# Forming the low parts of the down projection's weights with a ScalarE write and an accumulating DMA

## The chip, the cores and the metric

The kernel runs on one core of a Trainium2 chip. The metric is the device time in microseconds of one execution. Three runs of the kernel before took 1912.0, 1912.75 and 1913.21 us; the median is 1912.75 us.

## The reference

One layer of a decoder trunk is computed for 256 tokens of width 2048, in float32: a normalised input goes through one wide projection, a gated linear attention and a dilated attention run beside each other, their gated sum goes through an output projection and is added to x, and a SwiGLU block and a final norm follow. What matters here is the last part:

```
hf = _rmsnorm(x, ffn_norm[l])
gu = hf @ w_ffn_in[l]
gate, up = gu[..., :D_FF], gu[..., D_FF:]
x = x + (jax.nn.silu(gate) * up) @ w_ffn_out[l]
```

D_FF is 5632. The product with w_ffn_out, 5632 x 2048, is the down projection.

## The kernel before

Every large product is done in three passes of TensorE in a reduced 32-bit format (F32R). A weight w is split exactly in two parts, a high part wh (w rounded to the format) and a low part wl = w - wh; the activations have a high and a low part too. A product is high times high, high times low and low times high.

The weights are streamed from HBM. A *unit* is one DMA of 1 MB issued on SyncE's queue into one of three buffers `raw` (L167 to L173). A unit holds two *subs* of 512 KB, 128 partitions by 1024 elements. For each sub, `split` (L175 to L185) has ScalarE write wh from raw, and VectorE write wl as raw minus wh. The buffers wh and wl have five copies each (`LA + 1`, with `LA = 4`). The main loop splits sub i+4 and then multiplies with sub i (`next_split()` and `mains(sub)`, L899 to L915), so the write of sub i+4 has to wait until TensorE is done with sub i-1. When both subs of a unit are split, the unit's buffer is free and the next unit's load is issued (`next_split`, L839 to L845).

The work is a list of jobs, each one product with a block of weights 512 columns wide, in a fixed order. For the SwiGLU block the order is written out at L815 to L822: pairs of jobs with w_ffn_in (gate and up, functions `evac_fgate` and `evac_fup`), and in between three stretches of down jobs (`down`, L810). The first two stretches have four jobs of 8 subs, the last has four jobs of 6 subs: 32 + 32 + 24 = 88 subs. A sub of a down job is used by 12 matmuls: two 128-row tiles of the weights, two tiles of tokens, three passes.

The elementwise work on a finished job runs in its *evacuation*, which is called right after the split of the next job's fifth sub (index 4) and before that job's first matmul. An up job's evacuation occupies ScalarE and VectorE in turn (`fold`, the products with the gate, and the split of the result by `split_act`). The evacuation of a down job of the last stretch has VectorE add to x1, ScalarE square, and GpSimd multiply by the final norm's weights (L799).

The very last job is done one token tile after the other. It goes through its 6 subs with the first 128 tokens alone (6 matmuls per sub), then twice with half of the columns for the other 128 tokens. Its sixth sub (index 5) goes to blocks named h instead of the ring (L179). DMAs of small tensors are issued on GpSimd's queue.

Of the kernel before, what the change touches and what calls it, by code (L numbers as in the profile page):

```python
# [10 lines left out]
F32 = mybir.dt.float32  # L11
F32R = mybir.dt.float32r
AF = mybir.ActivationFunctionType
ALU = mybir.AluOpType
AX = mybir.AxisListType

P = 128
# [11 lines left out]


class HiLo:
    """Four feature tiles of [128, 256] as exact high and low parts, side by side."""

    def __init__(self, tiles):
        self.t = [t.rearrange("p (a w q) -> p a w q", a=2, w=2) for t in tiles]
# [9 lines left out]


class Job:
    """One product with a weight block.

    kind T gives [token, feature]; F and G give [feature, token], G with the product of the low  # L50
    part of the activations in its own half of the bank. `pairs` names the pairs of PSUM banks."""

    def __init__(self, kind, w, row0, nkt, col0, ncols, ktu, acts, evac, pre=None, pairs=None):
        self.pairs = pairs
# [6 lines left out]
def trunk_layer(ctx: ExitStack, tc: tile.TileContext, x, attn_norm, w_in, w_gk_up, b_gk, gla_norm,  # L61
                b_gate, w_branch_gla, w_branch_dil, w_out, ffn_norm, w_ffn_in, w_ffn_out, rel_bias,
                final_norm, onehot, out):
    nc = tc.nc
# [33 lines left out]
        return HiLo([block(tag, j, F32R) for j in (i, i + 1)])  # L98

    def split_act(hl, src):  # L100
        """Splits [128, 4, 256] in SBUF."""
        for i in range(2):
            act(hl.t[i][:, :, 0], src[:, 2 * i:2 * i + 2], AF.Copy)
        for i in range(2):
            nc.vector.tensor_sub(hl.t[i][:, :, 1], src[:, 2 * i:2 * i + 2], hl.t[i][:, :, 0].bitcast(F32))
# [5 lines left out]
    table = [None]  # L111
# [8 lines left out]
            need(func)  # L120
        nc.scalar.activation(o, i, func, **kw)  # L121

# [1 line left out]
    need(AF.Ln)  # L124
    grow = const.tile([16, P], F32, name="grow")
    nc.scalar.dma_start(grow, attn_norm[0].rearrange("(a p) -> a p", p=P))
# [16 lines left out]
    make_identity(nc, ident)  # L143
    epst = const.tile([P, 1], F32, name="epst")
    nc.vector.memset(epst, EPS)
# [1 line left out]
    def add(job):  # L147
        jobs.append(job)
        job.subs = []
# [25 lines left out]
    def split(sub):  # L175
        n, k = sub["job"].ncols, sub["k"]
        src = sub["unit"]["raw"][:, sub["s0"] * n:(sub["s0"] + k) * n]
        if sub["job"] is jobs[-1] and sub["idx"] > LA:
            wh, wl = (block("h", 2 * (sub["idx"] - LA) + i, F32R) for i in range(2))  # L179
        else:  # L180
            wh = ring.tile([P, 1024], F32R, name="wh", tag="wh", bufs=LA + 1)
            wl = ring.tile([P, 1024], F32R, name="wl", tag="wl", bufs=LA + 1)
        act(wh[:, :k * n], src, AF.Copy)
        nc.vector.tensor_sub(wl[:, :k * n], src, wh[:, :k * n].bitcast(F32))  # L184
        sub["w"] = [t[:, :k * n].rearrange("p (a n) -> p a n", a=k) for t in (wh, wl)]  # L185

    def mains(sub, only=None, part=None):
# [46 lines left out]
                    nc.tensor.matmul(dst, st, mv, start=first and i == 0 and j % per_bank == 0,  # L234
                                     stop=last and i == 2, skip_group_check=True)

# [1 line left out]
    queue = deque()  # L238

    def advance(n=1):  # L240
# [8 lines left out]
                return  # L249

    def idle(n):
        """From an elementwise part to the matmul part n steps later."""
        for _ in range(2 * n + 1):
            yield

# [5 lines left out]
            advance()  # L261

    def col_rstd(name, ss, n):
        """1 / sqrt(ss / n + eps) for a small tile, with one Newton step."""
        p, w = ss.shape
        v = const.tile([p, w], F32, name=f"v_{name}", tag=f"v_{name}")
        r = const.tile([p, w], F32, name=f"r_{name}", tag=f"r_{name}")
        t = const.tile([p, w], F32, name=f"t_{name}", tag=f"t_{name}")
        nc.vector.tensor_scalar(v, ss, 1.0 / n, EPS, op0=ALU.mult, op1=ALU.add)
        act(t, v, AF.Ln)  # L270
        act(r, t, AF.Exp, scale=-0.5)
        nc.vector.tensor_mul(t, r, r)
        nc.vector.scalar_tensor_tensor(t, t, -0.5, v, op0=ALU.mult, op1=ALU.mult)
        nc.vector.scalar_tensor_tensor(r, t, 1.5, r, op0=ALU.add, op1=ALU.mult)
        return r

    def row_bcast(name, r):
        """[128 tokens, 2] -> the same values along the free axis of all partitions."""
        pt = ps_b()
        for a in range(2):  # L280
            nc.tensor.transpose(pt[:, a * P:(a + 1) * P], r[:, a:a + 1].to_broadcast([P, P]), ident)
        R = const.tile([P, S], F32, name=name)
        nc.scalar.copy(R, pt[:, :S])
        return R

# [1 line left out]
    def scale_split(hl, pt, gcol, js=range(4)):  # L287
        for j in js:
            act(hl.hi(j), pt[j], AF.Copy, scale=gcol[:, j:j + 1])
# [5 lines left out]
        return [t[:, j * S:(j + 1) * S] for j in range(4)]  # L295

    def to_blocks(tiles, gcol, hl, js, pt):
        """Transposes the feature tiles js of [token, 2, 512], scales by feature and splits exactly."""
        for j in js:
            for a in range(2):  # L300
                nc.tensor.transpose(pt[j][:, a * P:(a + 1) * P], tiles[:, a, j * P:(j + 1) * P], ident)
        yield
        scale_split(hl, pt, gcol, js)
# [5 lines left out]

    env = {}  # L310

# [1 line left out]
    def fold(job, dst, R=None):  # L313
        """dst[:, j] = (high + low accumulator of feature tile j), times the row R of the tokens."""
        n = len(job.acc)
        for j in range(n):
            t = const.tile([P, S], F32, name="fold", tag="fold", bufs=2)
            act(t, job.acc[j][:, S:2 * S], AF.Copy)
            nc.vector.tensor_add(dst[:, j], job.acc[j][:, 0:S], t)
        if R:  # L320
            nc.vector.tensor_mul(dst, dst, env[R][:, None, :].to_broadcast([P, n, S]))
# [7 lines left out]
                                 env[R][:, None, :].to_broadcast([P, 2, S]))  # L329

    def view(key, slot, a, fresh=True):
        """Block `slot` under `key`, seen as [128, a, 1024 / a]."""
        if key not in env:
            env[key] = block("z", slot).rearrange("p (a t) -> p a t", a=a)
        return env[key]

# [1 line left out]
    gctx = ExitStack()  # L338
    gtmp = gctx.enter_context(tc.tile_pool(name="gtmp", bufs=1))
    wgk = gtmp.tile([17, 1024], F32, name="wgk")  # L340
# [7 lines left out]
    nc.vector.memset(inside[:, ::64], 0.0)  # L348

    def g_chunk(lo, hi, slots, base):  # L350
        """Evacuates output-gate columns lo..hi of a half: silu, and the low-rank part past 1024."""
        def go(job):
            for a in range(2):
                c = lo
                while c < hi:
                    sc = env["rstd"][:, a:a + 1]
                    if c >= 1024:
                        act(lrn[:, a], job.acc[a][:, c - lo:hi - lo], AF.Copy, scale=sc)
                        c = hi
                        continue  # L360
                    j = c // 512
                    e = min(hi, (j + 1) * 512)
                    g = view(("g", base + j), slots[j], 2)
                    act(g[:, a, c - j * 512:e - j * 512], job.acc[a][:, c - lo:e - lo],
                                         AF.Silu, scale=sc)
                    c = e
        return go
# [121 lines left out]
        scale_split(hl, [pt[:, f] for f in range(4)], cols[:, 48:52])  # L489
        oglaHL[h] = hl  # L490

# [1 line left out]
    odil = []  # L493
    dctx = ExitStack()
    ftab = dram.tile([8, 3, 384], F32, name="ftab")
# [117 lines left out]
                then()  # L613
        return go

# [1 line left out]
    h_acts = acts_of(hT)  # L617

    def win(kind, col, n, evac, pre=None):
# [28 lines left out]
        push("bias", bias_table())  # L648
    win("T", C_V + 512, 512, evac_t(("v", 1), 1, after_b))

# [1 line left out]
    SL = ((2, 3, 4, 5, 6), (7, 8, 9, 0, 1))  # L652
    for r in range(4):
        sl = SL[r % 2]
# [12 lines left out]
                    push(f"D{r}", dil_head(h, r))  # L667
            win("T", base + 2048, 256, evac_vd(r, g, sl[3 + g // 2], then if g == 2 else None))

# [1 line left out]
    merged = []  # L671

    def evac_gate(key, slot, bcol):
# [32 lines left out]
    turn = [0]  # L706

    def pairs(n):
        """The next n of the four pairs of PSUM banks."""
        p = [(turn[0] + i) % 4 for i in range(n)]  # L710
        turn[0] = (turn[0] + n) % 4
        return p
# [9 lines left out]
        add(Job("G", w_branch_dil, 0, 8, 512 * i, 512, 4, odil_acts, evac_branch(("gb", i), i, True),  # L722
                {0: lambda: drain("D3")}, **kw(False)))

# [1 line left out]
    x1 = []  # L726
    ss1 = const.tile([P, 2, 4], F32, name="ss1")
    ss2 = const.tile([P, 2, 5], F32, name="ss2")
# [37 lines left out]
        add(Job("T", w_out, 0, KT, 512 * c, 512, 4, merged_acts, evac_out(c),  # L766
                {0: reload_x} if c == 0 else None))

# [1 line left out]
    aT = {}  # L770

    def evac_fgate(p):
# [48 lines left out]
            down(4, 4, False)  # L821
    down(8, 3, True)  # L822

# [1 line left out]
    def rows_to_cols(r, n, name):  # L825
        pt = ps_b()
        nc.tensor.transpose(pt[:, 0:n], r, ident[0:n, 0:n])
# [86 lines left out]
        if sub["last"]:  # L914
            pending = sub["job"]  # L915

# [1 line left out]
    tot = const.tile([P, 2], F32, name="tot2")  # L918

    def add_tokens(src, a, q):  # L920
# [40 lines left out]


def _onehot():
    """Row of the bias table (32: masked) for each dilation and each distance -127..256."""
    import numpy as np
    hot = np.zeros((33, 3, 384), np.float32)
    for g, d in enumerate(DILS):
        for i in range(384):
            delta = i - 127
            b = 32  # L970
            if 0 <= delta <= 128 * d and delta % d == 0:
                dist = np.maximum(delta, 1).astype(np.float64)
                b = delta if delta < 16 else min(
                    31, 16 + int((np.log(dist / 16) / math.log(2048 / 16) * 16).astype(np.int64)))
            hot[b, g, i] = 1.0
    return hot
# [21 lines left out]
```

## Time and profile before

| what | value |
|---|---|
| median of three runs | 1912.75 us |
| span of the profiled execution, first to last instruction | 1911.5 us |
| TensorE busy | 1896.5 us, 99% of the span |
| VectorE busy | 1094.3 us, 57% |
| ScalarE busy | 907.1 us, 47% |
| GpSimd busy | 26.1 us, 1% |
| mean granted TensorE clock | 0.999 of full speed |
| bytes moved by DMA | 352.38 MB, mean 184 GB/s |

The page gives the span of the profiled execution and no separate time of its own for what lies outside it; the three runs without a profile are 0.5 to 1.7 us above the span. A busy share near 99% says that the engine had hardly a gap. The chain that ended last, followed back from the last instruction, is TensorE's for 99% of the span. The DMA share is the mean busy share of 16 DMA engines; a stretch can read slightly over 1.

### The profile page before, as it was taken

What the parts mean: (1) busy time and instruction counts of PE and PEld (TensorE: products, weight loads), DVE (VectorE), ACT (ScalarE), POOL (GpSimd) and SP (SyncE); (2) the same over time, 40 slices, a digit from 0 to 9 for tenths busy, and PEclk for the clock granted to TensorE, in tenths of its full rate; (3) what the DMA queues carried; (4) which work ended last, traced back from release to release, by engine and by line L of the source; (5) the groups of instructions that cost most, each with busy time, mean ns of one, the idle gap of its engine ahead of it and who ended that gap; (6) DMA issues with size and microseconds to landing.
All of it is one profiled execution on the core that took longest, in us unless ns stands there. A gap on an engine that the chain in (4) does not pass through costs nothing.

```text
span 1911.5 us, 26946 instructions
## 1 busy us (share of the span) xinstructions
PE 1896.5 (99%) x11190; PEld 1677.5 (88%) x11190; DVE 1094.3 (57%) x1294; ACT 907.1 (47%) x1233; POOL 26.1 (1%) x31
## 2 busy tenths in 40 slices
PE   8999999999999999999999999999999999999998
PEld 8988988899999999998888889888888888888886
DVE  6446646656565655555656655555555566645564
ACT  6446545544454444544545455444443444433443
POOL 0000000000000000000000000000000000000001
PEclk9999999999999999999999999999999999999999
DMA  7655555555555555455555755555555555565553
GB/s 242 206 196 165 166 182 171 158 171 185 178 174 188 178 177 181 152 185 196 178 175 178 270 191 177 177 192 199 181 198 191 183 176 177 189 209 197 183 184 119
DMA packets 218497, 352.38 MB, mean 184 GB/s; under 512 B 6011, under 2 KB 91095, under 8 KB 218376
## 3 DMA queue, kind: packets, MB, share of 16 engines
q1 hardware_dynamic: 214480, 346.18, 54.5%
q10 hardware_dynamic: 3320, 3.18, 0.6%
q8 instruction: 87, 1.43, 0.3%
q0 software_dynamic: 576, 1.31, 0.2%
q14 instruction: 34, 0.28, 0.0%
HBM read 348.52 MB, written 2.13 MB: 183 GB/s over the span
## 4 chain that ended last, share of the span: by engine, by line
PE 99%; DVE 0%; DMA 0%; ACT 0%; SPq 0%; issue 0%; DVEq 0%; ACTq 0%
PE acc L234 37%; PE acc L216 22%; PE acc L218 11%; PE psa L216 6%; PE psb L216 6%; PE psa L218 3%; PE psb L218 3%; PE psa L234 3%; PE psb L234 3%; PE psa L549 1%; PE psb L594 0%; PE psa L471 0%; PE psb L453 0%; DMA o<-in_x_dram 0%; PE psb L559 0%; PE psb L596 0%
## 5 line engine op out<-in xcount | busy, mean ns | idle before, releaser
L184 DVE TENSOR_TENSOR wl<-raw,wh 128x1024 fp32r<-128x1024 f32 (+2 forms) x655 | 788.2, 1215 | 716.4 <-ACT wh L121 706.5
L121 ACT ACTIVATE wh<-raw 128x1024 fp32r<-128x1024 f32 (+2 forms) x655 | 679.6, 1048 | 744.3 <-PE acc L234 287.2
L216 PE MATMUL acc<-h,wh 128*128 128x512 f32 x1600 | 568.1, 399 | 0.0
L218 PE MATMUL acc<-h,wl 128*128 128x256 f32 x1600 | 448.3, 280 | 0.0
L216 PEld LDWEIGHTS acc<-h,wh 128*128 128x128 f32 x1600 | 300.6, 188 | 74.3 <-issue 1.3
L234 PE MATMUL acc<-wh,h 128*128 128x256 f32 (+3 forms) x1344 | 312.1, 322 | 0.0
L218 PEld LDWEIGHTS acc<-h,wl 128*128 128x128 f32 x1600 | 302.0, 189 | 0.3
L234 PEld LDWEIGHTS acc<-wh,h 128*128 128x128 f32 x1344 | 227.4, 190 | 17.2 <-issue 1.6
L234 PE MATMUL acc<-wl,h 128*128 128x256 f32 (+3 forms) x672 | 214.9, 320 | 0.0
L234 PE MATMUL acc<-wh,z 128*128 128x512 f32 (+1 forms) x628 | 192.5, 386 | 0.0
L216 PE MATMUL psa<-h,wh 128*128 128x512 f32 x448 | 168.4, 399 | 0.0
L216 PE MATMUL psb<-h,wh 128*128 128x512 f32 x448 | 168.4, 399 | 0.0
L234 PE MATMUL acc<-h,wh 128*128 128x256 f32 x896 | 163.3, 284 | 0.0
L234 PEld LDWEIGHTS acc<-h,wh 128*128 128x128 f32 x896 | 139.9, 192 | 0.4
L234 PEld LDWEIGHTS acc<-wh,z 128*128 128x128 f32 x628 | 117.3, 188 | 23.7
L234 PEld LDWEIGHTS acc<-wl,h 128*128 128x128 f32 x672 | 127.9, 190 | 7.3
L234 PE MATMUL acc<-h,wl 128*128 128x256 f32 x448 | 126.7, 283 | 0.0
L218 PE MATMUL psa<-h,wl 128*128 128x256 f32 x448 | 125.8, 281 | 0.0
L218 PE MATMUL psb<-h,wl 128*128 128x256 f32 x448 | 125.8, 281 | 0.0
L234 PE MATMUL acc<-wl,z 128*128 128x512 f32 (+1 forms) x314 | 121.1, 386 | 0.0
L216 PEld LDWEIGHTS psb<-h,wh 128*128 128x128 f32 x448 | 84.2, 188 | 21.1
L216 PEld LDWEIGHTS psa<-h,wh 128*128 128x128 f32 x448 | 84.2, 188 | 21.0
(225 smaller groups left out, 1776.8 us busy)
## 6 DMA issues: line engine op xcount, KB each, us to landing
raw<-in_w_in_dram SPq DMA_DIRECT2D x144, 1024.0 KB, 5.1
raw<-in_w_ffn_in_dram SPq DMA_DIRECT2D x88, 1024.0 KB, 5.1
raw<-in_w_ffn_out_dram SPq DMA_DIRECT2D x44, 1024.0 KB, 5.1
raw<-in_w_branch_gla_dram SPq DMA_DIRECT2D x16, 1024.0 KB, 5.2
raw<-in_w_out_dram SPq DMA_DIRECT2D x16, 1024.0 KB, 5.0
raw<-in_w_branch_dil_dram SPq DMA_DIRECT2D x8, 1024.0 KB, 5.0
raw<-in_w_in_dram SPq DMA_DIRECT2D x8, 692.0 KB, 4.4
T<-ftab ACTq DMA_DIRECT2D x8, 384.0 KB, 5.5
```

The source lines that it names most:

```text
L121: nc.scalar.activation(o, i, func, **kw)
L184: nc.vector.tensor_sub(wl[:, :k * n], src, wh[:, :k * n].bitcast(F32))
L216: nc.tensor.matmul(job.acc[j], wh[:, kk, j * P:(j + 1) * P], hl.both(aj), start=first, stop=last, skip_group_check=True)
L218: nc.tensor.matmul(job.acc[j][:, 0:S], wl[:, kk, j * P:(j + 1) * P], hi, start=False, stop=last, skip_group_check=True)
L234: nc.tensor.matmul(dst, st, mv, start=first and i == 0 and j % per_bank == 0, stop=last and i == 2, skip_group_check=True)
L549: nc.tensor.matmul(p1[:, g * 256:(g + 1) * 256], qk[g][:, 0, 128:256], qk[g][:, 1], start=g != 1, stop=True, skip_group_check=True)
```

## The change

For weights of w_ffn_out alone, VectorE's subtraction is replaced. ScalarE writes wl as minus the rounded weights (the same Copy, with scale -1, from raw into the F32R buffer), and a DMA on GpSimd's queue reads the same 512 KB of weights from HBM once more and adds them to wl in SBUF. All other weights are split as before. The rest of the diff removes docstrings and comment lines, and lines after L185 move down by 8.

```diff
         act(wh[:, :k * n], src, AF.Copy)
-        nc.vector.tensor_sub(wl[:, :k * n], src, wh[:, :k * n].bitcast(F32))
+        if sub["job"].w is w_ffn_out:
+            job = sub["job"]
+            r0 = job.row0 + sub["k0"] * P
+            act(wl[:, :k * n], src, AF.Copy, scale=-1.0)
+            nc.gpsimd.dma_start(wl[:, :k * n].rearrange("p (a n) -> p a n", a=k),
+                                job.w[r0:r0 + k * P, job.col0:job.col0 + n].rearrange("(a p) n -> p a n", p=P),
+                                accum_op=ALU.add)
+        else:
+            nc.vector.tensor_sub(wl[:, :k * n], src, wh[:, :k * n].bitcast(F32))
```

ScalarE's instructions at the end of the program, before: the last six rows of splits belong to the last down jobs, junk is the square of the evacuated x1, and h_16356 is the high part of the very last sub.

```order
L121 ACTIVATE wh<-raw 128x1024 x6
L121 ACTIVATE junk,ss_99<-o_9995 128x512 x2
L121 ACTIVATE wh<-raw 128x1024 x5
L116 ACT_TABLE_LOAD
L121 ACTIVATE wh<-raw 128x1024
L121 ACTIVATE junk,ss_99<-o_9997 128x512 x2
L121 ACTIVATE h_16356<-raw 128x1024
L121 ACTIVATE junk,ss_99<-o_9999 128x256 x2
```

The same place with the change, from the load of the activation table on; h_16443 and h_16444 are the high and the low part of the very last sub.

```order
L116 ACT_TABLE_LOAD
L121 ACTIVATE wh<-raw 128x1024
L121 ACTIVATE wl<-raw 128x1024
L121 ACTIVATE junk,ss_99<-o_9997 128x512 x2
L121 ACTIVATE h_16443<-raw 128x1024
L121 ACTIVATE h_16444<-raw 128x1024
L121 ACTIVATE junk,ss_99<-o_9999 128x256 x2
```

Each write of a high part is now followed by a write of the low part on the same engine.

GpSimd's instructions from the loads of the final norm's weights to the end, before:

```order
L737 DMA o_10001<-in_final_norm_dram 128x1024
L737 DMA o_10003<-in_final_norm_dram 128x1024
L799 TENSOR_TENSOR o_9993<-o_9993,o_10001 128x512 x2
L799 TENSOR_TENSOR o_9995<-o_9995,o_10001 128x512 x2
L799 TENSOR_TENSOR o_9997<-o_9997,o_10003 128x512 x2
```

The same with the change; each DMA into wl or h_16444 is one accumulating transfer of 512 KB.

```order
L745 DMA o_10001<-in_final_norm_dram 128x1024
L745 DMA o_10003<-in_final_norm_dram 128x1024
L188 DMA wl<-in_w_ffn_out_dram 128x2x512 x75
L807 TENSOR_TENSOR o_9993<-o_9993,o_10001 128x512 x2
L188 DMA wl<-in_w_ffn_out_dram 128x2x512 x6
L807 TENSOR_TENSOR o_9995<-o_9995,o_10001 128x512 x2
L188 DMA wl<-in_w_ffn_out_dram 128x2x512 x6
L807 TENSOR_TENSOR o_9997<-o_9997,o_10003 128x512 x2
L188 DMA h_16444<-in_w_ffn_out_dram 128x2x512
```

There are 75 + 6 + 6 + 1 = 88 of these DMAs, and the last of them stands behind two products of GpSimd.

## Rows read from the trace of the kernel before

**Rows 1.** The page's first part: busy us, share of the span, instructions of each engine.
```profile
PE 1896.5 (99%) x11190; PEld 1677.5 (88%) x11190; DVE 1094.3 (57%) x1294; ACT 907.1 (47%) x1233; POOL 26.1 (1%) x31
```
**Rows 2.** Waits of TensorE: who waited for whom, us in total, times, longest.
```profile
PE psb L234 <- DVE h L184: 0.5, 1, 0.5
```
**Rows 3.** Chain that ended last, first and last down stretch: start us, us, work.
```profile
1391.09 43.55 PE acc L234 x192
1434.63 21.76 PE psa L234 x96
...
1869.25 16.33 PE psa L234 x72
```
**Rows 4.** Busy us by engine in the three down stretches; clock, DMA share, GB/s last.
```profile
1391.00:1478.00 87.00, 87.00 (x386) 72.03 (x385) 47.81 (x46) 36.11 (x38) 0.00 (x0) 1.00 0.57 194
...
1659.00:1746.00 87.00, 87.00 (x386) 71.97 (x385) 47.82 (x46) 36.07 (x38) 0.00 (x0) 1.00 0.56 194
...
1836.00:1885.00 49.00, 49.00 (x219) 40.59 (x218) 30.54 (x30) 24.95 (x33) 5.09 (x4) 1.00 0.50 172
```
**Rows 5.** The same view, microseconds within one burst of weight loads.
```profile
1404.00:1405.00 1.00, 1.00 (x6) 0.81 (x5) 0.80 (x1) 0.25 (x1) 0.00 (x0) 1.00 1.05 410
1405.00:1406.00 1.00, 1.00 (x6) 0.84 (x5) 0.16 (x1) 0.81 (x1) 0.00 (x0) 1.00 1.05 385
...
1407.00:1408.00 1.00, 1.00 (x6) 0.80 (x6) 0.07 (x1) 0.53 (x1) 0.00 (x0) 1.00 1.04 387
```
**Rows 6.** DMA issues: queue, count, KB each, median us from issue to landing.
```profile
raw<-in_w_ffn_out_dram SPq DMA_DIRECT2D x44, 1024.0 KB, 5.1
...
o<-in_final_norm_dram POOLq DMA_DIRECT2D x2, 512.0 KB, 5.6
...
oh<-in_onehot_dram POOLq DMA_DIRECT2D x3, 49.5 KB, 4.9
...
ftab<-fs POOLq DMA_DIRECT2D x3, 12.0 KB, 2.2
```
**Rows 7.** GpSimd's issue of the three onehot DMAs: ns min/median/max, first and last start.
```profile
L504 POOL DMA_DIRECT2D oh<-in_onehot_dram x3: 514/531/535, 349.3 to 350.4; - x3
```
**Rows 8.** Timeline at the start of the first down stretch: start us, us, engine, work, idle before.
```profile
1390.92 0.40 PE L234 MATMUL acc<-wh,z 128*128 128x512 f32 x1
...
1391.01 1.06 ACT L121 ACTIVATE wh<-raw 128x1024 fp32r<-128x1024 f32 x1 [1.77 <-PE psb L216]
...
1392.10 1.23 DVE L184 TENSOR_TENSOR wl<-raw,wh 128x1024 fp32r<-128x1024 f32 x1 [1.61 <-ACT wh L121]
...
1399.08 4.01 ACT L121 ACTIVATE wh<-raw 128x1024 fp32r<-128x1024 f32 x4
```
**Rows 9.** Timeline at the start of the very last job, same columns.
```profile
1885.41 0.39 PE L234 MATMUL psb<-wh,z 128*128 128x512 f32 x1
...
1885.61 1.06 ACT L121 ACTIVATE wh<-raw 128x1024 fp32r<-128x1024 f32 x1 [0.36 <-PE psa L234]
...
1887.84 1.28 DVE L794 TENSOR_TENSOR o<-psa,o 128x512 f32<-128x512 f32 x2
...
1888.56 0.63 ACT L121 ACTIVATE junk<-o 128x512 f32<-128x512 f32 x1 [1.89 <-DVE o L794]
...
1889.36 2.55 POOL L799 TENSOR_TENSOR o<-o,o 128x512 f32<-128x512 f32 x2 [13.78 <-ACT junk L121]
...
1889.95 1.05 ACT L121 ACTIVATE h<-raw 128x1024 fp32r<-128x1024 f32 x1
```
**Rows 10.** Busy us and granted clock after TensorE's last matmul, columns as in Rows 4.
```profile
1903.00:1904.00 1.00, 0.11 (x1) 0.00 (x0) 0.42 (x1) 0.33 (x2) 0.00 (x0) 1.00 0.00 0
...
1906.00:1907.00 1.00, 0.00 (x0) 0.00 (x0) 1.00 (x3) 0.43 (x1) 0.00 (x0) 0.97 0.03 10
1907.00:1909.00 2.00, 0.00 (x0) 0.00 (x0) 0.19 (x1) 0.00 (x0) 0.00 (x0) 0.50 1.01 378
```

## The prediction

> **What bounds the kernel now.** I read the engines' busy shares first: TensorE is busy for 1896.5 of 1911.5 us, the others for 57% at most [rows 1]. So work taken from VectorE cannot buy time by itself; it can only if TensorE waits for VectorE somewhere. The list of waits says how often it does: once, for 0.5 us, for the low part of the very last sub [rows 2]. The most that the change can gain is therefore 0.5 us. What it can lose depends on the three down stretches alone, the only place where it acts.
>
> There TensorE sets the pace. A job of 8 subs takes 21.76 us and one of 6 takes 16.33 us [rows 3], so a sub takes 2.72 us, and each sub needs 512 KB of weights in that time. TensorE is busy for the whole of each stretch; ScalarE for 36 of 87 us, VectorE for 48, the DMA engines for 0.57 of the time, moving 194 GB/s [rows 4]. That last pair is the one to look at: the DMA engines are the resource that the change loads most, and they are already more than half used.
>
> **The change part by part.**
>
> *Removed:* 88 subtractions on VectorE of 1.23 us [rows 8]. They are off the path but for the 0.5 us named, which I set at nothing, since a later arrival takes its place.
>
> *Added on ScalarE:* 88 writes like those of wh, 1.06 us each [rows 8]. A sub then takes 2.12 us of ScalarE against TensorE's 2.72 us. It fits, with 0.6 us to spare: in a non-last stretch nothing but one evacuation lies beside it. So in steady running ScalarE costs nothing; with that cover gone, it would cost at most 1.06 x 88 = 93 us. The loads of `raw` now wait for ScalarE's second write instead of VectorE's subtraction, at about the same moment (2.12 us after the first write starts, against 1.06 + about 0.03 + 1.23).
>
> *Added on GpSimd's queue:* 88 issues. An issue takes 0.53 us there [rows 7], well under 2.72. Each waits for ScalarE's write of its own wl; behind it on GpSimd are only the next such DMA and, in the last stretch, six products that nobody needs before the end.
>
> *Added on the DMA engines:* this is the large term. First the plain transfers. In a burst of weight loads the engines move 385 to 410 GB/s at a share of 1.04 to 1.05 [rows 5], so full use is about 387 GB/s, and the 512 KB (0.524 MB) of a sub cost 1.36 us of all 16 engines. (The stretch's 194 GB/s at 0.57 would make it 340 GB/s and 1.54 us; I take the saturated rows, since saturation is the question.) The accumulating transfer isn't in this trace. Bounds: it reads at least the same 512 KB from HBM, so it costs no less than another 1.36 us. A sub then takes 2.72 us of DMA, exactly TensorE's 2.72: just hidden. From above: the 512 KB transfers on GpSimd's queue land 5.6 us after issue [rows 6]; if only one were served at a time, a sub would take 5.6 us. In between, what an accumulation has to do says more than either end: it fetches two operands, the weights and the old wl, to write one result. If the engines are charged by what they fetch, that is two plain transfers, 2.72 us, and a sub costs 1.36 + 2.72 = 4.08 us of the engines. I take this value.
>
> The Trainium skill, "Collectives: The Full Stack", section "The bandwidth ceiling: the fold count and why AG ≠ RS ≠ AR", states that an adding transfer is slower not because of the addition but because it needs two source reads on the same read ring, and gives a measured ratio of 1.93 to a plain one. No run here shows that yet. By its ratio a sub would cost 1.36 + 2.62 = 3.98 us, and the sum below would be about 9 us smaller. The nearest row here, a plain transfer, says 2.72 us per sub and no loss of bandwidth at all; the two differ by over 100 us, and this rule speaks against the change.
>
> *Sum for the bandwidth.* (4.08 - 2.72) x 88 = 120 us. The buffers give little back: the four subs split ahead at a stretch's start are used up by the first landing. Only the last stretch has no next weights to load behind it; three raw buffers are then 6 subs, 6 x 1.36 = 8 us less.
>
> *Added wait: the landing.* Wherever the split is done late, the landing time of 5.6 us [rows 6] comes on top. At the start of a down stretch sub 4 is split at 1391.01, then the up job's evacuation holds ScalarE until 1399.08 [rows 8]. With the new write of sub 4 in front, that becomes 1400.1; the two writes of sub 5 end at 1402.3, and its DMA lands at 1407.9. TensorE, which starts the stretch at 1390.92, wants the low part of sub 5 after five subs and one matmul, at 1390.92 + 13.6 + 0.23 = 1404.8. That is 3.1 us late, three times: 9.3 us. These waits come while the DMA engines are behind anyway in the bandwidth case, so there they are part of the 120, and I do not add them.
>
> At the end they do add. In the very last job a sub lasts half as long, 1.36 us. Sub 4 is split from 1885.61 [rows 9], is written by 1887.73 and lands at 1893.3, against a need at 1885.41 + 4 x 1.36 + 0.23 = 1891.1: 2.2 us late. VectorE's adds no longer stand behind a subtraction, so the squares follow at 1887.7 to 1889.2, the two writes of sub 5 end at 1891.3, GpSimd's two products (2.55 us, [rows 9]) are done by then, and its DMA lands at 1896.9, against a need at 1892.4. Both together delay the end by 4.5 us; nothing else covers it, for all that follows waits for this product.
>
> The sum is 120 - 8 + 4.5 = 116 us on the profiled execution's span of 1911.5 us. The median of the runs lies 1.25 us above the span, outside the first and last instructions; I put that down as unchanged: 1912.75 + 116 = 2029 us.
>
> TensorE's clock I leave out of the sum. It stayed at full speed (the 2.4 GHz level) until 1906 us and fell to half after an idle stretch that began at 1903 [rows 10]; gaps of 1.36 us per sub are shorter than that one. A few longer waits at the starts of stretches could slow a few microseconds of matmuls.
>
> **The rivals.**
>
> *The transfer costs the engines no more than a plain one; only latency is left.* The DMA share would rise to about 1 without passing it, and the waits counted above remain: 9.3 + 4.5 = 13.8 us, 1926.5 us. For it: 2.72 against 2.72 us just fits, and if the read of wl in SBUF goes beside the read of HBM, it is free. Against it: no slack at all is left, and two operands are fetched.
>
> *The accumulating transfers are served one after the other, or slower still.* Then a sub takes the landing time: (5.6 - 2.72) x 88 = 253 us, with the tail 258, 2170 us. For it: an operation that reads, adds and writes back has a longer way to go than any in this trace. Against it: three small transfers issued on this queue 0.53 us apart [rows 7] had a median landing of 4.9 us each [rows 6], so they overlapped.
>
> *Not slower: everything is hidden.* If the transfer lands within 2.3 us (the 12 KB ones have a median of 2.2 us [rows 6]), sub 5 of a stretch arrives at 1404.6 before its need at 1404.8, and sub 4 of the last job at 1890.0 before 1891.1; only the last sub is late, at 1893.6 against 1892.4, in place of the 0.5 us of before. Then the time is 1912.75 + 0.7 = 1913.5 us, and with a still shorter landing up to 0.5 us under the median. It decides from a landing under 2.5 us. Against it: 512 KB landed in 5.6 us there, and 1 MB in 5.1 us on the other queue [rows 6]; at 387 GB/s the bytes alone take 1.36 us, with raw loads between them.
>
> **How the numbers follow.** Bandwidth with two reads: 0.53. Served singly or slower: 0.23. Latency alone: 0.17. Hidden: 0.07, of which 0.02 would be measured as faster. A measurement of this kernel tells a change from none at about 0.2%, 3.8 us; only the hidden case ends within it, and all others are slower: faster 0.02, same 0.05, slower 0.93. The likeliest case has its own range of 1969 to 2089 us (a charge of 1.5 to 2.5 plain transfers: 88 x (1.36 x 2.5 - 2.72) = 60 us and 88 x (1.36 x 3.5 - 2.72) = 180 us, less the last stretch's 8 and with the tail's 4.5). The range for the time takes in the latency case from 1922 us and the serial one up to 2185 us, and leaves out about 0.1 on either side: the hidden case and the faster half of the latency case's spread below, transfers slower than 5.6 us per sub above.
>
> **What would show it right or wrong.** In the profile after: the three down stretches take (4.08 x 88) = 359 us in place of 239, with a DMA share near 1 and near 390 GB/s or more, counting what is read from HBM and what from SBUF; TensorE's waits there are for the DMA into wl; a software queue carries 88 x 0.524 = 46 MB or twice that; the w_ffn_in stretches take as long as before. If the share stays under 0.9 while TensorE waits, it is not bandwidth but the service of single transfers, and the serial case holds. If TensorE waits only at the three starts and at the end, it is latency. The forecast is wrong if the stretches keep their 87 us, or if ScalarE (2.12 us per sub) shows as what TensorE waits for.

## The result and the profile after

The changed kernel takes 2022.89 us (2022.44 to 2024.03, four runs) against 1912.82 us for the kernel before beside it: a ratio of 1.0577, interval 1.0564 to 1.0589, 110 us slower. The profiled execution has a span of 2021.1 us, 109.6 us more than before.

First the page of the kernel after, its busy line, its DMA queues and the issues in the down projection (columns as in [rows 1] and [rows 6]; of a queue: packets, MB, share of 16 engines):

```profile
PE 1919.4 (95%) x11190; PEld 1672.1 (83%) x11190; DVE 986.8 (49%) x1206; ACT 989.8 (49%) x1321; POOL 130.2 (6%) x119
...
q1 hardware_dynamic: 214480, 346.18, 50.1%
q0 software_dynamic: 24512, 47.45, 12.7%
...
raw<-in_w_ffn_out_dram SPq DMA_DIRECT2D x44, 1024.0 KB, 14.6
wl<-in_w_ffn_out_dram POOLq DMA_DIRECT2D x87, 512.0 KB, 15.0
```

Against [rows 1] TensorE has fallen from 99% to 95%, and VectorE has lost its 88 subtractions. The load of a unit, 5.1 us before [rows 6], now takes 14.6 us to land, and the new transfers take 15.0. They have 88 x 0.524 = 46.1 MB, as announced.

The busy time by engine in the first two down stretches of the kernel after, then in a part of the last job in which nothing but accumulating transfers is left (columns as in [rows 4]):

```profile
1390.90:1519.30 128.40, 94.83 (x385) 69.35 (x384) 14.29 (x18) 61.99 (x66) 33.21 (x29) 1.00 1.07 259
1700.00:1828.70 128.70, 95.30 (x387) 69.68 (x386) 14.30 (x18) 62.49 (x66) 33.81 (x29) 1.00 1.07 258
...
1460.00:1470.00 10.00, 7.87 (x34) 5.90 (x33) 0.00 (x0) 4.46 (x5) 3.52 (x3) 1.00 1.09 262
...
1986.00:1996.00 10.00, 8.34 (x36) 6.01 (x34) 1.29 (x2) 8.53 (x11) 4.99 (x6) 1.00 1.13 206
```

These rows answer to [rows 4]. The 87 us of a stretch have become 128.7; TensorE is busy for 95 of them, at a granted clock of 1.00; the DMA share has gone from 0.57 to 1.07, a little above the 1.04 to 1.05 of the bursts in [rows 5]. So the engines are full, and yet they move 259 GB/s where full engines moved 385 to 410. (Counted with the second operand, the 0.524 MB of the old wl that each sub's addition works on in 4.02 us, the 259 become 389: the forecast's sign of near 390.) The last row says why: alone, accumulating transfers keep the engines full (1.13) with 206 GB/s, 0.53 of 387. One of 512 KB costs 0.524 / 0.206 = 2.55 us of all engines, 1.88 plain transfers. The page's queues say the same: q1 moved 346.18 MB in 50.1% of the engines' time and q0 its 46.1 MB in 12.5% (0.2% less for its small transfers, as before), which is 1.87 times as much per byte.

The waits of TensorE after (us in total, times, longest):

```profile
PE acc L242 <- DMA wl<-in_w_ffn_out_dram: 30.3, 26, 3.1
PE psa L242 <- DMA wl<-in_w_ffn_out_dram: 16.7, 15, 1.6
PE psb L242 <- DMA wl<-in_w_ffn_out_dram: 11.5, 11, 1.2
PE acc L242 <- ACT wh L121: 11.5, 11, 1.1
```

and two of them in the timeline, a sub apart, behind ScalarE's write of wh for the sub of the first:

```profile
1434.14 1.06 ACT L121 ACTIVATE wh<-raw 128x1024 fp32r<-128x1024 f32 x1 [2.03 <-PE acc L242]
...
1451.53 0.47 PE L242 MATMUL acc<-wl,z 128*128 128x512 f32 x1 [1.06 <-ACT wh L121]
...
1455.60 0.47 PE L242 MATMUL psa<-wl,z 128*128 128x512 f32 x1 [1.10 <-DMA wl<-in_w_ffn_out_dram]
```

At nearly every sub, the first matmul with a low part stands still. The view names ScalarE's wh in some of these waits; but ScalarE's wh for that sub was written some 16 us earlier, the matmul with wh before it had run, and the wait has the same length. It is the DMA there too: the rule that a wait for several semaphores is put down to the last one seen can misname it. All waits of this kind in the whole list sum to 88 us, and TensorE's busy time has risen by 22.9 us (1919.4 for 1896.5 in [rows 1]); together they are the 110.

### The profile page after: what moved, and what is told of

Same layout as the page of the kernel before. It is cut to its first block, busy times and chain, and to the rows that moved or that the text cites. A ratio compares the mean times of both kernels' runs of the same rounds, so it can differ in the third digit from the quotient of the medians.

```text
span 2021.1 us, 27240 instructions
## 1 busy us (share of the span) xinstructions
PE 1919.4 (95%) x11190; PEld 1672.1 (83%) x11190; DVE 986.8 (49%) x1206; ACT 989.8 (49%) x1321; POOL 130.2 (6%) x119
## 3 DMA queue, kind: packets, MB, share of 16 engines
q1 hardware_dynamic: 214480, 346.18, 50.1%
q0 software_dynamic: 24512, 47.45, 12.7%
## 4 chain that ended last, share of the span: by engine, by line
PE 69%; issue 17%; DMA 13%; POOL 1%; ACT 1%; DVE 0%; SPq 0%; POOLq 0%; DVEq 0%; ACTq 0%
PE acc L242 26%; PE acc L224 18%; DMA wl<-in_w_ffn_out_dram 12%; PE acc L226 9%; PE psa L224 4%; PE psb L224 4%; PE psa L226 2%; PE psb L226 2%; PE psb L242 1%; PE psa L242 1%; POOL wl L188 1%; ACT wh L121 1%; PE psa L557 1%; PE psb L602 0%; PE psa L479 0%
## 5 line engine op out<-in xcount | busy, mean ns | idle before, releaser
L192 DVE TENSOR_TENSOR wl<-raw,wh 128x1024 fp32r<-128x1024 f32 (+2 forms) x568 | 681.3, 1211 | 653.7 <-ACT wh L121 627.5
L242 PE MATMUL acc<-wl,z 128*128 128x512 f32 (+1 forms) x314 | 125.2, 399 | 42.8 <-DMA wl<-in_w_ffn_out_dram 30.3
L188 POOL DMA_DIRECT2D wl<-in_w_ffn_out_dram x87 | 103.4, 1188 | 803.5 <-ACT wl L121 787.5
L242 PEld LDWEIGHTS acc<-wl,z 128*128 128x128 f32 x314 | 59.2, 189 | 68.5 <-ACT wh L121 41.3
## 6 DMA issues: line engine op xcount, KB each, us to landing
raw<-in_w_ffn_out_dram SPq DMA_DIRECT2D x44, 1024.0 KB, 14.6
```

Of the source, the lines that this page charges most:

```text
L188: nc.gpsimd.dma_start(wl[:, :k * n].rearrange("p (a n) -> p a n", a=k), job.w[r0:r0 + k * P, job.col0:job.col0 + n].rearrange("(a p) n -> ...
```

## The experiments

**A plain copy in place of the addition.**

```diff
             nc.gpsimd.dma_start(wl[...], job.w[...],
-                                accum_op=ALU.add)
+                                )
```

> The DMA on GpSimd's queue copies the same 512 KB of weights into wl instead of adding them, so the low parts are not formed; everything else is as in the changed kernel. Theory (the DMA engines are charged for two operands of an addition): a copy fetches one, a sub costs 1.36 + 1.36 = 2.72 us of the engines against TensorE's 2.72, and only the waits for single landings are left: 1920 to 1945 us, stretches of 87 to 100 us. Rival (it is the number of transfers on GpSimd's queue, their issue of 1.19 us and their landing one behind the other, or ScalarE's second write): nothing of that changes, about 2020 us.

Measured: 1932.86 us, ratio 1.011 (1.0094 to 1.0127). In the middle of the first stretch (columns as in [rows 4]), the full engines move 381 GB/s and TensorE hardly waits:

```profile
1420.00:1470.00 50.00, 49.68 (x218) 40.10 (x217) 2.67 (x4) 36.31 (x38) 12.67 (x18) 1.00 1.17 381
```

Same queue, same number of transfers, same 46 MB read from HBM a second time, same writes by ScalarE, same F32R buffers: 90 of the 110 us are the addition alone. What is left is mostly latency: three waits at the starts (9.6 us in all), some 3 us of waits in the last job, and slow matmuls behind the three. TensorE's one long wait at the start of the first stretch, and the clock around it:

```profile
1406.56 0.76 PE L241 MATMUL acc<-wl,z 128*128 128x512 f32 x1 [3.13 <-DMA wl<-in_w_ffn_out_dram]
```

```profile
1401.00:1404.00 3.00, 2.43 (x11) 1.69 (x9) 0.00 (x0) 3.00 (x4) 1.02 (x2) 1.00 0.96 345
1404.00:1407.00 3.00, 0.44 (x1) 0.47 (x2) 0.00 (x0) 3.00 (x4) 1.08 (x2) 0.88 1.21 360
1407.00:1410.00 3.00, 3.00 (x9) 2.28 (x9) 0.00 (x0) 0.16 (x1) 0.71 (x1) 0.55 1.12 390
1410.00:1413.00 3.00, 3.00 (x15) 2.48 (x14) 0.00 (x0) 2.01 (x2) 0.00 (x0) 1.00 1.15 380
```

The wait of 3.13 us comes at the sub and with the size that the prediction gave (3.1 us); the other two stretches begin with 3.2 and 3.3 us. Behind it the granted clock is 0.55 for 3 us, near the 1.2 GHz level, and the row counts 9 matmuls where the next one counts 15: six of 0.23 us are some 1.4 us more per start.

**Two plain copies in place of one addition.**

```diff
-            nc.gpsimd.dma_start(wl[...], job.w[...], accum_op=ALU.add)
+            for t in (wl, env["fp"].tile([P, 1024], F32R, name="twin", tag="twin", bufs=4)):
+                nc.gpsimd.dma_start(t[...], job.w[...])
```

> In place of one accumulating DMA two copies of the same 512 KB, one into wl and one into a buffer that nobody reads; low parts are not formed. Theory (an addition is charged as two transfers, and nothing else of it matters): 1.36 x 3 = 4.08 us of the engines per sub, 2010 to 2045 us, the same as the changed kernel. Rival (the addition or the way back into SBUF costs something of its own): clearly faster than the changed kernel, under 1990 us.

Measured: 2024.97 us, ratio 1.059 (1.0574 to 1.0605), beside 2022.89 for the addition. The middle of its first stretch:

```profile
1420.00:1500.00 80.00, 60.50 (x239) 44.74 (x240) 4.04 (x6) 38.11 (x38) 27.96 (x40) 0.98 1.20 387
```

Three transfers of 512 KB per sub at 387 GB/s are 4.06 us; the addition and one plain transfer take 4.0. In time, an addition is two copies here, to within the 2 us between the two kernels.

**Additions of half the size.**

```diff
-            nc.gpsimd.dma_start(wl[...], job.w[...], accum_op=ALU.add)
+            nc.gpsimd.dma_start(wl[:, :n], job.w[r0:r0 + P, job.col0:job.col0 + n], accum_op=ALU.add)
+            nc.vector.tensor_add(wl[:, n:k * n], src[:, n:], wl[:, n:k * n].bitcast(F32))
```

> Of each sub's two row tiles the DMA adds the weights to the first alone (256 KB); VectorE adds them to the second from raw. Theory (charged by bytes fetched): an addition of 256 KB costs 2.55 / 2 = 1.28 us, a sub 1.36 + 1.28 = 2.64 us of the engines, just under TensorE's 2.72: stretches near 90 us, 1918 to 1940 us. Rival (each transfer costs a fixed time, whatever its size): as many transfers as in the changed kernel, so 2000 us or more.

Measured: 1932.72 us, ratio 1.0105 (1.009 to 1.012). As many additions as in the changed kernel, and the loss falls from 110 to 20 us. In steady running TensorE has no gap, though the engines are full:

```profile
1440.00:1470.00 30.00, 30.00 (x134) 24.86 (x133) 10.02 (x15) 22.16 (x24) 9.49 (x11) 1.00 1.06 282
```

The bytes decide, not the number of transfers, and 2.64 us of engines just fit under 2.72 us of TensorE.

**The addition's source in SBUF.**

```diff
-            nc.gpsimd.dma_start(wl[...], job.w[...], accum_op=ALU.add)
+            nc.gpsimd.dma_start(wl[:, :k * n], wh[:, :k * n], accum_op=ALU.add)
```

> The accumulating DMA adds wh from SBUF to wl instead of the weights from HBM, so HBM is read as often as in the kernel before, and wl becomes zero; the engines still fetch two operands for each result. Theory (the 16 engines are the limit): 1.36 + 2.55 us or a little less per sub, 1990 to 2025 us. Rival (reading HBM twice is the limit): 388 GB/s of reads fall back to 194, stretches near 90 us, 1918 to 1940 us.

Measured: 2005.17 us, ratio 1.0483 (1.0468 to 1.0499). Its queue of accumulating transfers, and what HBM gave:

```profile
q0 software_dynamic: 13248, 47.45, 11.8%
...
HBM read 348.52 MB, written 2.13 MB: 175 GB/s over the span
```

HBM gives the same 348.52 MB as in the kernel before, and 92 of 110 us stay. Its first stretch begins at 1389.33 and ends at 1509.82, 3.77 us per sub against 4.02. So reading HBM twice is not the limit. Why a sixth of the loss goes is open: the source lies nearer, but its rows are also longer (4 KB in place of 2 KB: 13248 packets on q0 in place of 24512, for the same 47.45 MB), and no run separates the two.

**One buffer less.**

```diff
-    NRAW, LA = 3, 4
+    NRAW, LA = 3, 3
```

> The changed kernel with three subs split ahead instead of four (LA = 3, four buffers of wh and wl). Theory (the DMA engines are full): a sub of a down stretch still takes 4.0 us, only fewer transfers queue, so the landing falls from 15 to about 11 us; down stretches of 128 to 133 us; in all 2020 to 2045 us, with some waits elsewhere since an up job's evacuation is as long as three subs. Rival (the loop of buffers: a landing of 15 us is what it is, and five buffers share 15 + 5.5 us, 4.1 us per sub): with four buffers 20.5 / 4 = 5.1 us per sub, stretches of 163 us, over 2100 us in all.

Measured: 2033.03 us, ratio 1.0634 (1.0619 to 1.0648). Its issues, and a stretch of its steady running:

```profile
raw<-in_w_ffn_out_dram SPq DMA_DIRECT2D x44, 1024.0 KB, 12.2
wl<-in_w_ffn_out_dram POOLq DMA_DIRECT2D x86, 512.0 KB, 10.8
```

```profile
1420.00:1500.00 80.00, 60.56 (x236) 45.07 (x235) 4.04 (x6) 40.11 (x40) 23.22 (x20) 0.96 1.09 256
```

The landing falls from 15.0 to 10.8 us, by about one sub's 4.0 us, and the rate stays (256 for 262 GB/s): the 15 us are a queue in front of full engines, not a latency that the buffers would have to cover. By this, more buffers should only lengthen the queue; no run has them. The 10 us more than in the changed kernel lie in the stretches too: the first two take 132.7 and 130.2 us, with longer gaps at their starts (last section).

**ScalarE's part alone.**

```diff
             act(wl[:, :k * n], src, AF.Copy, scale=-1.0)
-            nc.gpsimd.dma_start(wl[...], job.w[...], accum_op=ALU.add)
+            nc.vector.tensor_add(wl[:, :k * n], src, wl[:, :k * n].bitcast(F32))
```

> ScalarE still writes minus the weights, but VectorE adds the weights from raw, and no second DMA runs. Theory (ScalarE's 2.1 us per sub are hidden): 1911 to 1916 us; the end may come 1 us later. Rival (ScalarE's second write is a part of the loss): at each stretch's start and at the end the low part comes 1.06 us later, and 2.12 us of 2.72 leave little room: 1916 to 1930 us.

Measured: 1915.13 us, ratio 1.001 (1.0001 to 1.0019): 2 us, less than the 3.8 us that the prediction set as measurable, and all that ScalarE's 88 extra writes cost here. Its two large stretches take 87.1 us each, as before. The end is later; TensorE waits 1.7 us there instead of 0.5 [rows 2]:

```profile
PE psb L240 <- DVE h L188: 1.7, 1, 1.7
```

**The very last job without the DMA.**

```diff
-        if sub["job"].w is w_ffn_out:
+        if sub["job"].w is w_ffn_out and sub["job"] is not jobs[-1]:
```

> The changed kernel, but the very last job's six subs are split by VectorE as before. Theory: six transfers of 4.0 us go, and with them the waits of the last job: its first pass falls from 14.3 to about 8.7 us, and the last of the job before, whose splits ahead now need no transfer, gains up to 3 us: 2022.9 - 9 = 2014 us (2008 to 2018). Rival (the last job only takes over a backlog that lies in the DMA engines anyway): 2020 to 2023 us.

Measured: 2017.27 us, ratio 1.0544 (1.0529 to 1.0558): 5.6 us less than the changed kernel. The tail is a loss of its own; the gain lies nearer to the tail's 5.4 us (below) than to the 9 that were expected. The job before did not gain the 3 us: the last job begins here at 1989.91, and at 1989.58 in the changed kernel.

```profile
1989.91 0.39 PE L242 MATMUL psb<-wh,z 128*128 128x512 f32 x1
```

**Half-size additions, none where they come late.**

```diff
-        if sub["job"].w is w_ffn_out:
+        if (sub["job"].w is w_ffn_out and sub["job"] is not jobs[-1]
+                and not (sub["job"].col0 == 0 and sub["idx"] in (5, 6, 7))):
```

(on top of the half-size edit)

> As the run with the additions of half size, but the subs 5 to 7 of each stretch's first job and the whole last job are split by VectorE. Theory (what is left of the loss there, 20 us, is single landings that come late: three of 3 us at the starts, 4 us at the end, and the matmuls at half clock right after each): all of it goes, 1912 to 1917 us. Rival (it is ScalarE's load or the fuller DMA engines all along the stretches): 1922 us or more.

Measured: 1915.8 us, ratio 1.0016 (1.0007 to 1.0025). TensorE's waits in the last stretch:

```profile
PE acc L242 <- DMA wl<-in_w_ffn_out_dram: 3.0, 2, 2.5
PE psb L242 <- DVE h L192: 0.5, 1, 0.5
```

The first two stretches take 87.1 us each, with 58 of the 75 additions that are left in them. Of 20 us, 17 are gone, and the 3.0 us left lie in the last stretch, whose jobs have 6 subs: only its sub 5 was spared, and the next ones wait. So the remainder of the half-size run was single late landings, not ScalarE and not fuller engines.

## Why the prediction was right, point by point

- *The sum.* 2029 us were forecast and 2022.89 measured. Of the 6 us between them each of the three stretches has some 1.8, as the points below show.
- *TensorE bounds, and VectorE's 88 subtractions buy nothing.* Right: DVE is 107.5 us less busy, and nothing came of it.
- *A sub's plain load costs 1.36 us of all engines, an addition two of these, and a sub 4.08 us.* Right in the mechanism, a little large: the addition measured 2.55 us (1.88), a sub 4.0 us at 262 GB/s. The forecast for a stretch of 32 subs was 130.6 us; the two took 128.8 and 128.7. Taken from a sub's 4.02 us instead, an addition has 2.66 us (1.96). The Trainium skill ("Collectives: The Full Stack", section "The bandwidth ceiling: the fold count and why AG ≠ RS ≠ AR") has 1.93, measured between a collective that adds and one that only copies; the 1.88 and 1.96 of this trace lie on either side of it, and the sum by that ratio, 2020 us, is 3 us off where the one on record is 6 off. The choice between 2.72 and 5.6 us per sub, which no row of before could make, was the one that mattered, and it was made by argument. The run with two copies shows the equality in time; that it is the reading side of the engines that is charged is still argued.
- *The waits at the three starts, 3.1 us each, are part of the bandwidth's loss.* Right: in the first stretch no wait stands out from the others, and TensorE waits from its second sub on, so the subs split ahead buy next to nothing. In the last stretch a wait of 3.08 us does stand at sub 5, the place and size forecast; but sub 4 before it did not wait, and the five subs up to it still came 4.05 us apart on average. With plain copies the waits stand alone as 3.1, 3.2 and 3.3 us.
- *The last stretch saves 8 us of loads and loses 4.5 us at the end.* Near in size, but not in all of the mechanism. Its 24 subs took 92.7 us, from the first such matmul at 1919.08 to the last at 2011.79, where 97.9 - 8 + 4.5 = 94.4 had been forecast. The very last job of the kernel after begins and ends with these two groups of matmuls, the second from the chain that ended last:

```profile
1989.58 0.39 PE L242 MATMUL psb<-wh,z 128*128 128x512 f32 x1
```

```profile
2008.35 4.33 PE acc L242 x36
```

That is 23.1 us to the end of the second. Before, it began at 1885.41 [rows 9], and its last group was this one, 17.7 us:

```profile
1898.80 4.33 PE acc L234 x36
```

The difference is 5.4 us for a forecast of 4.5. The forecast had single landings that come late, the one of sub 4 by 2.2 us and the one of sub 5 after it. The trace has a wait at each of the subs 1 to 5 of the first pass; the first, the fourth and the last of them are

```profile
1992.08 0.47 PE L242 MATMUL psb<-wl,z 128*128 128x512 f32 x1 [0.76 <-DMA wl<-in_w_ffn_out_dram]
...
1999.70 0.47 PE L242 MATMUL psb<-wl,z 128*128 128x512 f32 x1 [0.92 <-DMA wl<-in_w_ffn_out_dram]
...
2002.64 1.40 PE L242 MATMUL psb<-h,z 128*128 128x512 f32 x5 [1.32 <-DMA h<-in_w_ffn_out_dram]
```

From sub 1 to sub 4 they come 2.54 us apart, the 2.55 us that one addition takes of full engines, in a pass that wants a sub every 1.36 us. So the rate of the additions, which the forecast left out of this pass, paces most of the tail, and only the last 2.94 us are longer than that. That 4.5 came near 5.4 is in part luck. The last landing is late as forecast, and later: the chain that ended last shows it 6.65 us after its issue, not 5.6, and issued at 1995.86, when GpSimd had ended the two products that the prediction took to be done by then.
- *ScalarE at 2.12 us per sub is hidden.* Right, shown by the run with its part alone (2 us, at the end).
- *GpSimd's issue takes 0.53 us.* Wrong in size: an accumulating issue takes 1.19 us, a plain one of the same shape 0.71. Both are under 2.72, so in steady running nothing hung on it; at the end one of 1.19 us stands before the two products in the chain that ended last:

```profile
L188 POOL DMA_DIRECT2D wl<-in_w_ffn_out_dram x87: 1161/1189/1624, 1381.4 to 1992.6; - x87
```

- *The clock is left out.* Right for the changed kernel: with gaps near 1.1 us it was 1.00 in two stretches. In the last it fell once, after the wait of 3.08 us, for a few microseconds, as the prediction allowed for:

```profile
1939.57 0.47 PE L242 MATMUL acc<-wl,z 128*128 128x512 f32 x1 [3.08 <-DMA wl<-in_w_ffn_out_dram]
```

```profile
1940.00:1945.00 5.00, 5.00 (x17) 3.91 (x16) 1.38 (x2) 1.00 (x2) 0.00 (x0) 0.66 1.09 262
```

But the latency rival was priced without it: its 13.8 us became 20 with the plain copy, in part since the matmuls after a wait of 3.1 us ran slowly.
- *The rivals.* Serial service is refuted by the landing of 15 us at 4.0 us per sub (four are under way at once). "Hidden" is refuted by the shares. "Latency alone" is what the plain copy shows.

The stretches have grown by 41.7 + 41.6 + 26.9 = 110.2 us, which is the whole difference of the spans (109.6): nothing was lost elsewhere, and the two w_ffn_in stretches between them take 180.9 and 90.4 us as before.

## What to carry to other kernels

Before work is moved to the DMA engines, add up their time in the stretch where it lands, at the rate of a saturated row, not by their busy share: here a sub's 2.72 us had room for one more plain transfer of 1.36 us and no more (with the plain copy TensorE was busy for 49.68 of 50 us), and an accumulating one costs nearly two. A landing time read under load can be a queue, so ask whether it shrinks with fewer transfers in flight before adding buffers. And where the bandwidth fits, look for the places at which the look-ahead has just been used up, the starts of stretches and the end: there the landing comes on top.

## What the runs showed of the hardware

- Accumulating transfers of 512 KB into SBUF moved 206 GB/s on full engines, plain ones 381 to 387; with the source in SBUF, in longer rows, a sub still cost 3.77 us.
- The DMA share reads 1.07 to 1.21 when two queues keep the engines full, so 1 is not its end.
- The granted clock was 0.55 after the wait of 3.13 us and 0.66 after the one of 3.08. In the run with one buffer less, three gaps of 3.5 to 3.8 us came some 17 us apart at the start of the first stretch, the clock behind one of them (below) was 0.83 over 10 us, and 1420 to 1500 us ran at 0.96. The gaps of 1.1 us of the changed kernel, one every 4 us, left it at 1.00:

```profile
1412.97 0.47 PE L242 MATMUL acc<-wl,z 128*128 128x512 f32 x1 [3.53 <-DMA wl<-in_w_ffn_out_dram]
```

```profile
1411.00:1421.00 10.00, 7.55 (x25) 5.84 (x26) 0.00 (x0) 3.16 (x4) 2.36 (x2) 0.83 1.10 252
```
